# A hybrid decoder step on one core: packed low-rank products, one merged item per head pair, a centred output weight, and an order made anew

## The chip, the cores and the metric

The kernel runs on one core of one Trainium2 chip. The metric is the device time of one execution in microseconds (us). Five engines work side by side: TensorE (PE in the profile, its weight loads PEld), VectorE (DVE), ScalarE (ACT), GpSimd (POOL) and SyncE (SP, which issues nearly all DMA transfers). Each engine has its own list of instructions, in the order in which the program gives them, and instructions of different engines wait for each other by semaphores.

## The reference, cut to what matters

One layer of a decoder is applied to a prompt of 1024 tokens and to 8 single-token samples, all in float32. The projection, the two recurrent branches and the merge are:

```python
p = jnp.einsum('btd,dn->btn', x, w_in)                     # 1024 -> 3088 + 4224 + 2048 columns
q, k, v, g_a, a_lr = _split(p_gla, GLA_SPLITS)             # gated linear attention (GLA), 4 heads
o_gla, S_gla = _gla_chunked(...)                           # then RMS norm, times silu(g_a)
w = jnp.exp(-RWKV_DECAY_SCALE * jax.nn.sigmoid(rwkv_w0 + jnp.tanh(w_lr) @ rwkv_w2))
a = jax.nn.sigmoid(rwkv_a0 + aa_lr @ rwkv_a2)              # low-rank products, rank 64
y, S_rwkv = _rwkv7_scan(r, w, k, v, kk, a, S_rwkv0)        # 16 heads of 64, a recurrence over tokens
m = sigmoid(gate_a) * (o_gla @ w_up_gla) + sigmoid(gate_b) * (o_rwkv @ w_up_rwkv)
out = m @ w_out
y_out = _layernorm(DEEPNORM_ALPHA * x + out, ln_g, ln_b, LN_EPS)
```

The outputs are `y_out` for prompt and samples, and the new states of both branches.

## The kernel before, in words

**Arithmetic.** A product of the projection kind is made of three matmuls in the type `fp32r`: the activations and the weights are each split into a high part (a cast on ScalarE) and a low part (a subtraction, mostly on VectorE), and high*high, high*low and low*high are added up in one PSUM bank. The tiles are `xs` (activations) and `wpart` (weights). Smaller products are plain float32; the profile counts two records for one such matmul.

**Stages.** The prompt is cut into two passes: the first has 512 tokens and the 8 samples (token tiles of 256 and 264), the second 512 tokens. For each pass a list of "blocks" of 128 columns of `w_in` is projected; each block takes 24 matmuls for a token tile (8 slices of the contraction times 3). Between them stand the two branches: the RWKV branch works on pairs of heads (`pair`: `front`, `back`, `turn`, `chain`, `norm`), the GLA branch on heads (`gla_head`). Behind the projections come the up-projections with the gates (`up_row`), and last `out`: the product with `w_out` in tiles of 128 tokens by 512 columns (`out`), then the residual and the layer norm (`out_part`). The weights `w_out` are loaded and split ahead of that by `load_out`, from row 0 to row 1023 in eight slices.

**Places that the change touches.** `warm` issues two matmuls on a tile of zeros before the first load has landed. `run_all` holds the order of the first loads (`self.first`): `wa`, `x0`, `w0`, `x1` and so on, all on SyncE. `low_rank` makes the 16 columns of the GLA decay with `wa`, four slices of the contraction side by side in the array. `lora_sample` makes the samples' two low-rank products in two halves of 512 columns: four items, each one matmul with 64 rows and 8 columns, each with its own copy and store. In `back`, the inverse of a triangular block is merged in two products: `pA` (32 small matmuls) and `pZ` (4 matmuls, in the profile `big<-X,A`); `turn` then transposes the tiles b and k (16 transposes, `big<-cons,bk`) as an item of its own.

**Tiles of the array.** A matmul with few rows or columns uses only a part of the 128x128 array; the profile writes the part as rows*columns (128*32, 64*128).

**What sets the order.** A list scheduler in the kernel (`Order`) writes the instruction order of all engines when the program is built. Every piece of work is a generator ("stream") that offers one instruction, or one group of them (`together`), at a time; `price` gives each a duration, `HOP` the delay from one engine to another, `SWITCH` the price of another tiling of the array, and the stream whose next item can start first (less a priority) is written next. PSUM banks are taken from four classes: `proj` (2 banks), `big` (4), `pch` (1), `pY` (1). A new price moves instructions on all engines.

Of the kernel before, what the change touches and what calls it, by code (L numbers as in the profile page):

```python
# [20 lines left out]
P = 128  # L21
D = 1024
# [40 lines left out]
WARM = 2  # L63
# [3 lines left out]
HOP = {"P": 0.2, "D": 0.26, "G": 0.14, "V": 0.14, "A": 0.14}  # L67
# [78 lines left out]
def price(eng, name, out, args, ins):  # L146
# [3 lines left out]
    if eng == "P":  # L150
# [4 lines left out]
        if args[0].dtype == F32R:  # L155
            return max(m / 1200, n / 2165)
        if rows == cols == P:
            return 2 * max(m, n) / 1200 + 0.005
# [98 lines left out]
class Order:  # L257
# [4 lines left out]
    def __init__(self, nc):  # L262
        self.P, self.A, self.V, self.G, self.S, self.E, self.C = (Engine(**e) for e in (
            {"P": nc.tensor}, {"A": nc.scalar}, {"V": nc.vector}, {"G": nc.gpsimd}, {"S": nc.sync},
            {"V": nc.vector, "G": nc.gpsimd}, {"A": nc.scalar, "V": nc.vector}))
        self.tiles = (P, P)
# [157 lines left out]
class Kern(Order):  # L424
# [72 lines left out]
    def setup(self):  # L497
# [20 lines left out]
        nc.scalar.preload_act_table_set(EXP)  # L518
# [47 lines left out]
    def warm(self):  # L566

        z = self.kept["XT"][0]
        ps = yield from self.bank("big", [P, 512])
        for _ in range(WARM):  # L570
            yield self.P.matmul(ps, z[:, :P], z[:, :512], start=True, stop=True)
        self.free(ps)
# [41 lines left out]
    def load_x(self, src, i, wait=None, low_rank=False):  # L614
# [9 lines left out]
        def high():  # L624
            for k in range(NK):
                yield lambda: len(raws) > k
                h, lo = yield from self.get("xs", 2)
                yield self.A.copy(h[:, :n], raws[k])
# [3 lines left out]
        def low():  # L632
            for k in range(NK):
                yield lambda: len(his) > k
                yield self.E.tensor_sub(los[k], raws[k], his[k].bitcast(F32))
# [12 lines left out]

    def load_w(self):
# [5 lines left out]
        def high():  # L655
            n = 0
            while True:
                yield lambda: len(raws) > n
                w = yield from self.get("wpart")
                yield self.A.copy(w[:, 0], raws[n][0])  # L660
# [5 lines left out]
        def low():  # L666
            for n in range(count):
# [3 lines left out]
                yield self.E.tensor_sub(w[:, 1], raw, w[:, 0].bitcast(F32))  # L671
# [10 lines left out]
        for n, (src, c0, j, i) in enumerate(todo):  # L682
# [356 lines left out]
    def lora_sample(self, lw, l2s):  # L1039
        for hf, l2 in enumerate(l2s):  # L1040
            for q in range(2):
                rs = slice(64 * q, 64 * q + 64)
                pw = yield from self.bank("big", [NS, 512])
                yield self.P.matmul(pw, lw[rs, HT:], l2[rs], start=True, stop=True)
                wa = yield from self.row(512)
                yield self.A.copy(wa[:NS], pw)
                self.free(pw)
                yield self.S.dma_start(self.WA[q, :, 512 * hf:512 * hf + 512], wa[:NS])
                self.free(wa)
            self.free(l2)  # L1050
# [77 lines left out]
    def front(self, c, p, st, d):  # L1128
# [63 lines left out]
        for x in range(0, NCH, H):  # L1192
# [3 lines left out]
                            for n in range(H) for h, hs in enumerate(HS)])  # L1196
# [45 lines left out]
    def back(self, d):  # L1242
# [5 lines left out]
        for h in range(2):  # L1248
# [3 lines left out]
                                      start=True, stop=True) for n in range(2) for x in range(H) for h in range(2)], 2.0)  # L1252
# [4 lines left out]
        pZ = yield from self.bank("big", [P, H, 32])  # L1257
        yield together([self.P.matmul(pZ[q[g]], A_[:, q[g]], d.X2[:, g], start=True, stop=True) for g in range(4)])
# [6 lines left out]
        self.free(pZ, A_, d.X2)  # L1265

    def turn(self, d):

        bt = d.BK.rearrange("p c t -> p (c t)")[:, :2 * HT].rearrange("p (c h k) -> p c h k", c=NCH, h=2)
        pt = yield from self.get("big", 2)  # L1270
        yield together([self.tr(pt[h][:, x * C:x * C + C], d.BK[hs, x, h * C:h * C + P])
                        for x in range(NCH) for h, hs in enumerate(HS)])
# [14 lines left out]
    def chain(self, c, p, d):  # L1287
# [12 lines left out]
        for x in range(NCH):  # L1300
# [20 lines left out]
            for h, hs in enumerate(HS):  # L1321
# [3 lines left out]
                else:  # L1325
# [5 lines left out]
                        for x in range(first, NCH) for h, hs in enumerate(HS)], 0.5)  # L1331
        yield together([self.P.matmul(pY[h][HS[x % 2], x // 2], GG[:, x, 1, h], u_[:, x, h], start=False, stop=(x >= NCH - 2))
                        for h in range(2) for x in range(NCH)])
# [211 lines left out]
    def load_out(self):  # L1545
# [4 lines left out]
        for j in range(2):  # L1550
            for hf in range(2):
                yield self.S.dma_start(self.lnv[j][hf], self.a["ln"][j, 512 * hf:512 * hf + 512].partition_broadcast(P))
        for k in range(NK):
# [273 lines left out]
```

## Time and profile before

| | |
|---|---|
| time, median of 3 runs | 1467.58 us (1467.34 to 1470.01) |
| profiled execution | 1466.08 us |
| its span, first to last instruction | 1464.1 us |
| PE busy | 1443.8 us, 99% of the span |
| DVE, ACT, POOL busy | 1139.0, 888.7 and 77.7 us |
| DMA | 318.06 MB, mean 217 GB/s |

The profiled execution takes 2.0 us more than its span, which is what lies around the first and last instruction. In the profile's rows, `x8` counts instruction records, numbers behind a bar are busy time and the mean of one in ns, and `<-` in brackets names what ended the idle time before the row. In a timeline a row merges neighbouring instructions of one kind: its start, the time that it covers, and their count.

### The profile page before, as it was taken

What the parts mean: (1) busy time and instruction counts of PE and PEld (TensorE: products, weight loads), DVE (VectorE), ACT (ScalarE), POOL (GpSimd) and SP (SyncE); (2) the same over time, 40 slices, a digit from 0 to 9 for tenths busy, and PEclk for the clock granted to TensorE, in tenths of its full rate; (3) what the DMA queues carried; (4) which work ended last, traced back from release to release, by engine and by line L of the source; (5) the groups of instructions that cost most, each with busy time, mean ns of one, the idle gap of its engine ahead of it and who ended that gap; (6) DMA issues with size and microseconds to landing.
All of it is one profiled execution on the core that took longest, in us unless ns stands there. A gap on an engine that the chain in (4) does not pass through costs nothing. (4 is left out here: it accounts for less than half of the span.)

```text
span 1464.1 us, 32120 instructions
## 1 busy us (share of the span) xinstructions
PE 1443.8 (99%) x11670; PEld 1261.4 (86%) x11670; DVE 1139.0 (78%) x3022; ACT 888.7 (61%) x2356; POOL 77.7 (5%) x107
## 2 busy tenths in 40 slices
PE   9999999999999999999999999999999999999997
PEld 6999999999989998878888887878787899988786
DVE  6687879788988798877778898797876866755665
ACT  6666767777776776665855565566456746553210
POOL 0000000001100001000000010111000000000000
PEclk9999999999999999999999999999999999999999
DMA  9786887587767877667566556655564777896432
GB/s 314 275 276 212 265 285 233 198 282 267 230 226 233 281 237 240 209 193 224 151 188 209 156 187 205 201 140 187 181 180 138 251 221 244 294 319 230 131 113 82
DMA packets 201273, 318.06 MB, mean 217 GB/s; under 512 B 81827, under 2 KB 97068, under 8 KB 201116
## 3 DMA queue, kind: packets, MB, share of 16 engines
q1 hardware_dynamic: 201116, 316.01, 67.2%
q8 instruction: 93, 1.52, 0.4%
q14 instruction: 64, 0.52, 0.1%
HBM read 197.32 MB, written 118.61 MB: 216 GB/s over the span
## 5 line engine op out<-in xcount | busy, mean ns | idle before, releaser
L218 PE MATMUL proj<-xs,wpart 128*128 128x264 f32 (+2 forms) x5640 | 1018.3, 327 | 1.0 <-DVE row L218 0.8
L218 PEld LDWEIGHTS proj<-xs,wpart 128*128 128x128 f32 x5640 | 807.4, 189 | 78.6 <-issue 9.2
L218 ACT CAST wpart<-wraw 128x512 fp32r<-128x512 f32 x210 | 129.8, 623 | 85.1 <-PE big L218 37.2
L218 DVE TENSOR_TENSOR row<-row 128x512 f32<-128x512 f32 (+8 forms) x331 | 169.6, 521 | 8.3 <-ACT row L218 2.6
L218 DVE TENSOR_TENSOR wpart<-wraw,wpart 128x512 fp32r<-128x512 f32 x203 | 141.7, 700 | 34.5 <-ACT wpart L218 32.6
L218 ACT ACTIVATE row<-row 128x512 f32<-128x512 f32 (+5 forms) x197 | 119.0, 607 | 17.8 <-DVE row L218 8.2
L218 PE MATMUL big<-xs,wpart 128*128 128x512 f32 (+2 forms) x576 | 102.9, 332 | 0.3
L218 DVE TENSOR_TENSOR X<-X,Xt 128x60 f32<-128x60 f32 (+21 forms) x432 | 95.5, 221 | 9.2
L218 DVE TENSOR_TENSOR Xt<-X,wide 128x60 f32<-128x60 f32 (+21 forms) x432 | 91.5, 212 | 8.8
L218 PEld LDWEIGHTS big<-xs,wpart 128*128 128x128 f32 x576 | 87.0, 188 | 11.8 <-DVE xs L218 1.1
L218 ACT ACTIVATE row<-proj,omu 128x256 f32<-128x256 f32 (+1 forms) x99 | 54.1, 547 | 69.3 <-PE proj L218 68.7
L218 DVE SCALAR_TENSOR_TENSOR wide<-pch,pc,s0p 64x64 f32<-64x64 f32 x208 | 58.7, 282 | 45.5 <-PE pch L218 40.0
L218 POOL TENSOR_TENSOR row<-row 128x512 f32<-128x512 f32 (+6 forms) x46 | 49.9, 1090 | 631.2 <-DVE row L218 279.9
L218 ACT COPY rh<-pch 128x128 f32<-128x128 f32 x101 | 26.9, 266 | 79.6 <-PE pch L218 78.6
L218 DVE SCALAR_TENSOR_TENSOR row<-proj,pv,row 128x255 f32<-128x255 f32 (+1 forms) x99 | 56.4, 570 | 21.9 <-ACT tail L218 14.2
L402 ACT ACT_TABLE_LOAD x56 | 71.8, 1283 | 0.9
L218 ACT COPY row<-big 128x128 f32<-128x128 f32 (+7 forms) x141 | 40.9, 311 | 51.8 <-PE big L218 39.2
L218 PE MATMUL big<-row 128*32 128x32 f32 (+4 forms) x1068 | 67.9, 237 | 1.1 <-DVE row L218 0.5
L218 ACT COPY row<-wide 64x64 f32<-64x64 f32 x240 | 58.2, 242 | 3.1
L218 PEld LDWEIGHTS pch<-wide,gg 128*128 128x128 f32 x256 | 43.2, 188 | 12.1 <-PE proj L218 4.6
L218 PE MATMUL pch<-wide,gg 128*128 128x128 f32 x256 | 50.9, 280 | 2.0 <-DVE wide L218 1.3
L218 ACT ACTIVATE row<-proj 128x128 f32<-128x128 f32 (+4 forms) x136 | 37.1, 326 | 25.8 <-PE proj L218 24.9
(265 smaller groups left out, 1991.0 us busy)
## 6 DMA issues: line engine op xcount, KB each, us to landing
w<-wpart SPq DMA_DIRECT2D x146, 512.0 KB
wpart<-w SPq DMA_DIRECT2D x146, 512.0 KB
wraw<-w_in SPq DMA_DIRECT2D x146, 256.0 KB
wide<-LD SPq DMA_DIRECT2D x16, 512.0 KB
wraw<-w_up_gla SPq DMA_DIRECT2D x32, 256.0 KB
wraw<-w_up_rwkv SPq DMA_DIRECT2D x32, 256.0 KB
sg<-row SPq DMA_DIRECT2D x16, 260.0 KB
row<-sg SPq DMA_DIRECT2D x16, 260.0 KB
```

The costliest lines, as they stand in the source:

```text
L218: ways.append((eng, lambda call=call: call(out, *args, **kw), price(eng, name, out, args, ins)))
L402: self.nc.scalar.preload_act_table_set(self.table)
```

## The change

- **Low-rank products of the samples** (`lora_sample`): the four matmuls become one item of four matmuls that sit in different parts of the array (two halves of the rows, two groups of 32 columns). Each takes 32 columns instead of 8, of which the last 8 are used. There are two copies instead of four, and four stores as before.
- **Second merge product and transposes as one item** (`back`, `turn`): `pZ` and the 16 transposes are given to the scheduler as one group, which takes three banks of `big` at once. `turn` only copies the result.
- **Start**: the warm-up is one matmul of 512 and one of 256 columns instead of two of 512. The first weights (`w0`) are loaded by ScalarE's own queue, ahead of the activation table; `x0` is issued ahead of `wa` on SyncE. The first x tile and the first weight tile are split in two pieces each. The first two blocks may take PSUM banks of `pY` and `big` too.
- **End** (`load_out`, `out`, `residual`, `out_part`): each row of `w_out` has its mean subtracted when it is split, and the residual is scaled and its mean subtracted by a stream of its own as soon as x has landed, so the sum has mean zero without a subtraction of its own. The product with `ln_g` is made before the variance is known. In the last tile, ScalarE scales by the inverse deviation where GpSimd did, and GpSimd has one product and one sum left. `load_out` loads two slices of `w_out` ahead.
- **Prices of the scheduler**: `HOP` for VectorE 0.14 -> 0.21 and ScalarE 0.14 -> 0.22, ScalarE's fixed part 0.097 -> 0.04, small changes for PE, and factors on four groups (1.1, 2.7, 0.66, 1.17) and on the merged one (0.72).

```diff
-WARM = 2
+WARM = (512, 256)
-HOP = {"P": 0.2, "D": 0.26, "G": 0.14, "V": 0.14, "A": 0.14}
+HOP = {"P": 0.2, "D": 0.26, "G": 0.14, "V": 0.21, "A": 0.22}
...
-            return max(m / 1200, n / 2165)
+            return max(m / 1200, 0.005 + n / 2260)
...
-        return 0.097 + n / 1200 + (0.042 if len(src) == len(ins) else 0.0) + 0.094 * extra
+        return 0.04 + n / 1200 + (0.042 if len(src) == len(ins) else 0.0) + 0.094 * extra
...
-            yield from self.load(f"w{n}", self.S.dma_start(raw, src[c0 // P, j]))
+            yield from self.load(f"w{n}", (self.S if n else self.B).dma_start(raw, src[c0 // P, j]))
+            if not n:
+                self.nc.scalar.preload_act_table_set(EXP)
...
-                    banks.append((yield from (self.get("proj") if b.src is self.a["w_in"] else self.get_of("proj", "pY", "big"))))
+                    banks.append((yield from (self.get("proj") if b.src is self.a["w_in"] and at > 1 else self.get_of("proj", "pY", "big"))))
...
     def lora_sample(self, lw, l2s):
...
+        m = slice(HT + NS - 32, HT + NS)
+        pw = yield from self.get("big", 2)
+        yield together([self.P.matmul(pw[q][32 * hf:32 * hf + 32], lw[64 * q:64 * q + 64, m], l2s[hf][64 * q:64 * q + 64],
+                                      start=True, stop=True) for hf in range(2) for q in range(2)], 2.0)
...
-        pZ = yield from self.bank("big", [P, H, 32])
-        yield together([self.P.matmul(pZ[q[g]], A_[:, q[g]], d.X2[:, g], start=True, stop=True) for g in range(4)])
+        pZ_, *pt = yield from self.get("big", 3)
+        pZ = pZ_[:, :H * 32].rearrange("p (c t) -> p c t", t=32)
+        yield together([self.P.matmul(pZ[q[g]], A_[:, q[g]], d.X2[:, g], start=True, stop=True) for g in range(4)]
+                       + [self.tr(pt[h][:, x * C:x * C + C], d.BK[hs, x, h * C:h * C + P])
+                          for x in range(NCH) for h, hs in enumerate(HS)], 0.72)
...
+            for hf in range(2):
+                yield self.V.tensor_reduce(m[:, hf:hf + 1], raw[hf], mybir.AxisListType.X, ALU.add)
+            yield self.V.tensor_scalar(m[:, 2:3], m[:, 0:1], m[:, 1:2], -1.0 / D, ALU.add, ALU.mult)
...
-                yield self.A.copy(hi, raw)
-                yield self.E.tensor_sub(lo, raw, hi.bitcast(F32))
+                yield self.A.activation(hi, raw[hf], AF.Identity, bias=m[:, 2:3])
+                yield self.V.scalar_tensor_tensor(lo, raw[hf], m[:, 2:3], hi.bitcast(F32), ALU.add, ALU.subtract)
...
+    def residual(self, z, st, x0, w):
+        for j in range(2):
+            yield self.S.dma_start(z[j], self.a["x"][x0:x0 + w, 512 * j:512 * j + 512])
+        for j in range(2):
+            yield self.V.bn_stats(st[:, 6 * j:6 * j + 6], z[j])
+        yield self.V.bn_aggr(st[:, 24:26], st[:, :12])
+        yield self.V.tensor_scalar(st[:, 26:27], st[:, 24:25], -ALPHA, None, ALU.mult)
+        for j in range(2):
+            yield self.A.activation(z[j], z[j], AF.Identity, scale=ALPHA, bias=st[:, 26:27])
...
             if aside:
-                yield G.tensor_scalar(y, y, mv[:, 0:1], rs, ALU.subtract, ALU.mult)
-                yield G.tensor_mul(y, y, lw)
+                yield A.activation(y, y, AF.Copy, scale=rs)
                 yield G.tensor_add(y, y, lb)
             else:
-                yield V.scalar_tensor_tensor(y, y, mv[:, 0:1], lw, ALU.subtract, ALU.mult)
                 yield V.scalar_tensor_tensor(y, y, rs, lb, ALU.mult, ALU.add)
...
-        self.first = ["wa", "x0", "w0", "x1", "x2", "x3", "w1", "x4", "x5", "x6", "x7", "pv", "shift", "w2", "w3", "cst"]
+        self.first = ["x0", "w0", "wa", "x1", "x2", "x3", "w1", "x4", "x5", "x6", "x7", "pv", "shift", "w2", "w3", "cst"]
```

What this does to the order of the instructions is shown at three places.

TensorE, the samples' low-rank products (`big<-row 8x512`, each a quarter of them) in the first pass, before, among the projections (`proj`):

```order
L218 MATMUL proj<-xs,wpart 128x256
L218 MATMUL big<-row 8x512
L218 MATMUL proj<-xs,wpart 128x256 x9
L218 MATMUL big<-row 8x512
L218 MATMUL proj<-xs,wpart 128x256 x7
L218 MATMUL big<-row 8x512
```

The same place in the changed kernel:

```order
L218 MATMUL proj<-xs,wpart 128x264 x24
L218 MATMUL proj<-xs,wpart 128x256 x15
L218 MATMUL big<-row 32x512 x4
L218 MATMUL proj<-xs,wpart 128x256 x9
L218 MATMUL proj<-xs,wpart 128x264 x24
```

The four products stood apart, with 9, 7 and 17 projection matmuls between them; now they stand together, once.

TensorE, one head pair of the first pass, before: `X,gg` is the first merge product, `X,A` the second, `cons,bk` the transposes of b and k, `cons,row` those of v.

```order
L218 MATMUL proj<-xs,wpart 128x264 x9
L218 MATMUL big<-X_173,A 32x128 x4
L218 MATMUL proj<-xs,wpart 128x256 x11
L218 MATMUL big<-cons,bk 128x64 x16
L218 MATMUL proj<-xs,wpart 128x256 x3
L218 MATMUL big<-cons,row 128x128 x4
```

A head pair of the first pass in the changed kernel:

```order
L218 MATMUL big<-X_5208,gg 32x32 x16
L218 MATMUL proj<-xs,wpart 128x256 x11
L218 MATMUL big<-X_172,A 32x128 x4
L218 MATMUL big<-cons,bk 128x64 x16
L218 MATMUL proj<-xs,wpart 128x256
L218 MATMUL proj<-xs,wpart 128x264 x18
L218 MATMUL big<-cons,row 128x128 x4
```

The projections that stood between the second product and the transposes stand elsewhere; this holds for all 16 pairs.

VectorE, the last tile of the output (`XT` holds residual and sum, `az` the vectors of the layer norm, `st` the statistics), before:

```order
L218 SCALAR_TENSOR_TENSOR XT_169<-XT_169,proj 128x256
L218 BN_STATS st<-XT_169 128x6
L218 BN_AGGR st<-st 128x2
L218 SCALAR_TENSOR_TENSOR XT_169<-XT_169,st,az 128x512 x2
L218 SCALAR_TENSOR_TENSOR XT_169<-XT_169,st,az 128x256 x2
```

and in the changed kernel:

```order
L218 TENSOR_TENSOR XT_168<-XT_168,az 128x512
L218 BN_STATS st<-XT_168 128x6
L218 TENSOR_TENSOR XT_168<-XT_168,az 128x256
L218 BN_STATS st<-XT_168 128x6
L218 BN_AGGR st<-st 128x2
L218 SCALAR_TENSOR_TENSOR XT_168<-XT_168,st,az 128x512
L218 SCALAR_TENSOR_TENSOR XT_168<-XT_168,st,az 128x256
```

Behind the last statistics stood four instructions and stand two; the products with `az` (`ln_g`) have gone ahead of them.

More of the change, by code (lines that the diff above doesn't have):

```diff
@@ L569, in warm @@
         ps = yield from self.bank("big", [P, 512])
-        for _ in range(WARM):
-            yield self.P.matmul(ps, z[:, :P], z[:, :512], start=True, stop=True)
+        for n in WARM:
+            yield self.P.matmul(ps[:, :n], z[:, :P], z[:, :n], start=True, stop=True)
         self.free(ps)
@@ L627, in high @@
                 h, lo = yield from self.get("xs", 2)
-                yield self.A.copy(h[:, :n], raws[k])
+                for s in self.halves(k or i or not low_rank, HT // 2, n):
+                    yield self.A.copy(h[:, s], raws[k][:, s])
                 his.append(h[:, :n])
@@ L634, in low @@
                 yield lambda: len(his) > k
-                yield self.E.tensor_sub(los[k], raws[k], his[k].bitcast(F32))
+                for s in self.halves(k or i or not low_rank, HT // 2, n):
+                    yield self.E.tensor_sub(los[k][:, s], raws[k][:, s], his[k][:, s].bitcast(F32))
                 if not low_rank:
@@ L647, in load_x, with halves @@
             raws.append(raw)
+    def halves(self, later, at, n):
+        return [slice(0, n)] if later else [slice(0, at), slice(at, n)]
     def load_w(self):
@@ L659, in high @@
                 w = yield from self.get("wpart")
-                yield self.A.copy(w[:, 0], raws[n][0])
+                for s in self.halves(n, P, 4 * P):
+                    yield self.A.copy(w[:, 0, s], raws[n][0][:, s])
                 his.append(w)
@@ L1039, in lora_sample @@
     def lora_sample(self, lw, l2s):
[L1040 to L1050, printed above, removed]
+        m = slice(HT + NS - 32, HT + NS)
+        pw = yield from self.get("big", 2)
+        yield together([self.P.matmul(pw[q][32 * hf:32 * hf + 32], lw[64 * q:64 * q + 64, m], l2s[hf][64 * q:64 * q + 64],
+                                      start=True, stop=True) for hf in range(2) for q in range(2)], 2.0)
+        self.free(*l2s)
+        for q in range(2):
+            wa = yield from self.row(512)
+            yield self.A.copy(wa[:64], pw[q][:64])
+            self.free(pw[q])
+            for hf in range(2):
+                yield self.S.dma_start(self.WA[q, :, 512 * hf:512 * hf + 512], wa[32 * hf + 32 - NS:32 * hf + 32])
+            self.free(wa)
     def tails(self):
@@ L1264, in back @@
             yield self.C.copy(GG[hs, :, 0, h], d.AZ[hs, :, 0])
-        self.free(pZ, A_, d.X2)
+        self.free(pZ_, A_, d.X2)
+        d.pt = pt
     def turn(self, d):
         bt = d.BK.rearrange("p c t -> p (c t)")[:, :2 * HT].rearrange("p (c h k) -> p c h k", c=NCH, h=2)
-        pt = yield from self.get("big", 2)
-        yield together([self.tr(pt[h][:, x * C:x * C + C], d.BK[hs, x, h * C:h * C + P])
-                        for x in range(NCH) for h, hs in enumerate(HS)])
+        pt = d.pt
         for h in range(2):
@@ L1552, in load_out, with load @@
                 yield self.S.dma_start(self.lnv[j][hf], self.a["ln"][j, 512 * hf:512 * hf + 512].partition_broadcast(P))
+        raws = []
+        def load():
+            for k in range(NK):
+                yield lambda: k - len(self.wo) < 2
+                raw = yield from self.rows(2, 512)
+                for hf in range(2):
+                    yield self.S.dma_start(raw[hf], self.a["w_out"][k * P:(k + 1) * P, 512 * hf:512 * hf + 512])
+                raws.append(raw)
+        self.spawn(load(), "out")
         for k in range(NK):
@@ L1600, in out @@
             z = [z_[ro, :512], z_[ro, 512:]]
-            for j in range(2):
-                yield self.S.dma_start(z[j], self.a["x"][x0:x0 + w, 512 * j:512 * j + 512])
             st = yield from self.get("st")
+            self.spawn(self.residual(z, st[ro], x0, w), "evacuate")
             end = fin and c.i
@@ L1753, in run_all @@
         self.ups = 0
+        self.levelled = set()
         self.plan, self.xq, self.ws, self.wo, self.gts, self.l2s = [], [], [], [], [], []
```

40 lines of the change are left out of this document (26 added, 14 removed).

## The prediction

> **What bounds the kernel now.** I read the page's first part first:
>
> ```profile
> span 1464.1 us, 32120 instructions
> PE 1443.8 (99%) x11670; PEld 1261.4 (86%) x11670; DVE 1139.0 (78%) x3022; ACT 888.7 (61%) x2356; POOL 77.7 (5%) x107
> ```
>
> TensorE is busy 99% of the span; only 20.3 us are not covered by a matmul. So time can go in three ways only: fewer or cheaper matmuls, less waiting on TensorE, and less before its first and behind its last matmul. VectorE and ScalarE count where TensorE waits for them. What TensorE waited for stands in the view of waits (total us, times, longest); of its sixteen rows the ones that I use:
>
> ```profile
> PE big L218 <- POOL XT L563: 1.7, 1, 1.7
> PE pch L218 <- DVE wide L218: 1.6, 5, 0.4
> ...
> PE big L218 <- issue: 1.2, 1, 1.2
> ...
> PE proj L218 <- DVE row L218: 0.8, 1, 0.8
> ...
> PE big L218 <- DMA X<-XD: 0.5, 1, 0.5
> ...
> PE big L218 <- ACT bk L218: 0.2, 1, 0.2
> ```
>
> The sixteen add up to 11.4 us. The 1.7 and the 0.8 (of the block wait) belong to the start, so 8.9 us of waits are spread over the other 1440 us, none over 1.2. That is all that a better order can remove.
>
> **The change part by part.** *Samples' low-rank products.* The timeline of TensorE has one of the four items, and, much later, an item whose four matmuls of 512 columns already stand side by side (128*16, eight records):
>
> ```profile
> 27.36 1.02 PE L218 MATMUL big<-row 64*8 64x512 f32 x2
> 28.32 1.33 PE L218 MATMUL proj<-xs,wpart 128*128 128x256 f32 x9
> ...
> 590.35 1.05 PE L218 MATMUL big<-row,wa 128*16 128x512 f32 x8
> 591.33 0.39 PE L218 MATMUL proj<-xs,wpart 128*128 128x264 f32 x1
> ```
>
> One item keeps the projections off for 28.32 - 27.36 = 0.96 us; four of them take 3.84. Four matmuls packed by columns take 591.33 - 590.35 = 0.98, no more than one alone. The new item is packed by two column groups and two row halves. If both run side by side it costs 0.98 and saves 2.9 us; if the row halves take turns, 1.96, and it saves 1.9. I take 2.9: the transposes quoted next run in two row halves, and 16 of them fit into 0.65 us.
>
> *Second merge product and transposes as one item.* One pair, then a place where an item of the tiling 128*32 is already followed at once by the transposes, then dense matmuls of 256 columns:
>
> ```profile
> 254.90 0.42 PE L218 MATMUL big<-X,A 128*32 128x128 f32 x8
> 255.26 1.56 PE L218 MATMUL proj<-xs,wpart 128*128 128x256 f32 x11
> 256.74 0.71 PE L218 MATMUL big<-cons,bk 64*128 64x64 f32 x16
> 257.39 0.39 PE L218 MATMUL proj<-xs,wpart 128*128 128x256 f32 x1
> ...
> 192.96 0.64 PE L218 MATMUL big<-row 128*32 128x256 f32 x8
> 193.53 0.76 PE L218 MATMUL big<-cons,bk 64*128 64x64 f32 x16
> 194.22 0.44 PE L218 MATMUL big<-cons,S 128*128 128x128 f32 x2
> ...
> 1450.62 0.87 PE L218 MATMUL proj<-gg,xs 128*128 128x256 f32 x6
> 1451.34 0.52 PE L218 MATMUL proj<-wide,xs 128*128 128x256 f32 x3
> ```
>
> Dense matmuls of 256 columns follow each other after (1451.34 - 1450.62)/6 = 0.12 us. The eleven between the two items should take 1.32 and took 256.74 - 255.26 = 1.48: the return to the full array and the next departure cost 0.16 together. Merging removes one return and one departure per pair and puts one change of tiling between the two. The transposes take 257.39 - 256.74 = 0.65 behind projections and 194.22 - 193.53 = 0.69 behind another tiling, so that change is not free. I take 0.1 per pair, 1.6 us for 16; the ends are 0 (the inner change costs what both outer ones did) and 0.16, that is 2.6 us. Nothing is queued behind a new wait that was not there: the transposes need b and k, which are older than the product's operand. What is new is that three of the four `big` banks must be free at once; that is a rival below.
>
> *Start.* SyncE, ScalarE, VectorE and TensorE in the first 16 us:
>
> ```profile
> 0.74 0.38 SPq L218 DMA_DIRECT2D wa<-wa  x1
> 1.18 0.42 SPq L218 DMA_DIRECT2D row<-xT  x1
> 1.74 3.78 PE L218 MATMUL big<-XT 128*128 128x512 f32 x4 [1.74 <-POOL XT L563]
> 3.98 0.62 ACT L218 CAST xs<-row 128x520 fp32r<-128x520 f32 x1 [1.97 <-DMA row<-xT]
> 4.95 0.62 ACT L218 CAST wpart<-wraw 128x512 fp32r<-128x512 f32 x1 [0.34 <-DMA wraw<-w_in]
> 5.62 1.59 PE L218 MATMUL proj<-xs,wpart 128*128 128x256 f32 x7
> 7.14 1.37 PE L218 MATMUL big<-row,wa 128*16 128x256 f32 x16
> ...
> 12.86 1.31 DVE L218 TENSOR_TENSOR wpart<-wraw,wpart 128x512 fp32r<-128x512 f32 x2 [0.30 <-ACT wpart L218]
> 15.60 0.85 PE L218 MATMUL proj<-xs,wpart 128*128 128x256 f32 x5 [0.77 <-DVE row L218]
> ```
>
> The first projection at 5.62 waits for the cast of `w0` (4.95 + 0.62) and for the warm-up (1.74 + 3.78 = 5.52). With x0 one issue slot earlier (1.18 - 0.74 = 0.44), `w0` beside it from ScalarE's queue (issue and table load are over before the first cast at 3.98), and casts of a half and a quarter, it could start near 4.5. But the low-rank item at 7.14 waits for x1 to x3, which move by about one slot. I take 0.5 for this part; the ends are 0 and 1.1. The wait of 0.77 ahead of 15.60 is block 1 waiting for a `proj` bank; with banks of `pY` and `big` it goes, and what is late next is the split of `w2` and `w3`, done at 12.86 + 1.31 = 14.17, in time. I take 0.9 with the refill behind it, ends 0 and 0.9. Together 1.4 (0 to 2.0).
>
> *Weighing a rule.* The warm-up runs at half pace: its four records take 3.78/4 = 0.95 us each, where the two of the same width at 27.36 take 0.48, while the page's clock row shows nothing of it. The Trainium skill, "TensorE: Matmul & The Clock Gate", Part 1, says that the array's clock is halved until some 3.4 us of sustained work have passed, whatever the number of matmuls. The rows agree as far as they go: the old warm-up of 3.78 us is over that, and the projections behind it run at full pace. By that rule a warm-up of 512 and 256 columns, an estimated 2 x 0.95 + 2 x 0.48 = 2.9 us, leaves part of the first real work at half pace, and the sum would be up to 1.8 us smaller (the rival on the clock).
>
> *End.* Behind the last matmul, and the costs of single instructions there, with the nearest row for ScalarE's scaling of 256 columns:
>
> ```profile
> 1457.74 2.98 DVE L218 SCALAR_TENSOR_TENSOR XT<-XT,st,az 128x512 f32<-128x512 f32 x4
> 1458.07 0.20 ACT L218 ACTIVATE st<-st 128x1 f32<-128x1 f32 x1
> 1459.50 2.17 SPq L218 DMA_DIRECT2D y_p<-XT  x3
> 1459.70 1.61 POOL L218 TENSOR_TENSOR XT<-XT,az 128x256 f32<-128x256 f32 x2
> ...
> L218 DVE SCALAR_TENSOR_TENSOR XT<-XT,st,az 128x512 f32<-128x512 f32 x2 | 1.6, 806 | 0.1
> L218 DVE SCALAR_TENSOR_TENSOR XT<-XT,st,az 128x256 f32<-128x256 f32 x2 | 1.3, 650 | 0.0
> ...
> 14.50 0.47 ACT L218 ACTIVATE row<-proj,omu 128x256 f32<-128x256 f32 x1 [0.80 <-PE proj L218]
> ```
>
> GpSimd ends at 1459.70 + 1.61 = 1461.31 and the third store's issue at 1461.67; the span ends 2.4 us later. In the changed kernel the deviation is known at 1458.27; VectorE's two instructions end at 1459.1 and 1459.75; ScalarE (0.47) and one GpSimd sum (1.61/2 = 0.8) end at 1459.55. Three issues of 0.43 each from 1459.1 end at 1460.4: 1.3 us saved (0.8 if GpSimd and VectorE hinder each other more, 1.8 if the issues overlap).
>
> *The rest costs nothing on TensorE's path.* The mean of `w_out` adds 16 reductions and 8 small instructions on VectorE, the residual stream one statistic per half tile; a pass over 512 columns takes 0.69, and the table loads grow by 8 of 1.28:
>
> ```profile
> 1434.82 0.69 DVE L218 BATCH_NORM_STATS2 st<-XT 128x6 f32<-128x512 f32 x1
> L402 ACT ACT_TABLE_LOAD x56 | 71.8, 1283 | 0.9
> ```
>
> VectorE gains about 16 x 0.69 = 11 us of work in the last 200 us and ScalarE 10 us overall; their idle shares (22% and 39%) cover it. Without cover it would delay the first output tile by one slice of `w_out`, 2 us.
>
> *The new order.* A new set of prices moves waits about. VectorE's later hand-over (0.07) speaks against the five `pch` waits; a place behind a swap of activations where two chain matmuls now stand with nothing between them speaks for one new wait of about 1 us. I take 1 us saved of the 8.9, with ends of 8.9 saved and 6 lost.
>
> Sum: 2.9 + 1.6 + 1.4 + 1.3 + 1.0 = 8.2 us. Against the profiled execution (1464.1 of span and 2.0 around it, 1466.1) that gives 1457.9. The median of the runs shown lies 1.5 us above that execution, so I forecast 1459 for the median.
>
> **The rivals.**
> - *The new order is worth far more than 1 us.* For it: the waits are many, small and of one kind. Against it: 8.9 us is the ceiling. With 6 of 8.9 saved and the merge at 2.6, the sum is 14.2: 1453.
> - *The new order gives back what the parts save.* TensorE's list is full and every place has moved; the waits would have to grow from 8.9 to about 15. For it: the new wait named above. Against it: the longest now is 1.2, and projections stand around nearly every item. With 6 lost instead of 1 saved the sum is 1.2: 1466, no change that can be told.
> - *Slower: the merged item stands in TensorE's list without its banks or its operand.* Three of four `big` banks at once must be emptied by ScalarE and VectorE, and the projections behind wait with it, 16 times. Without its own 1.6 the rest saves 6.6, so it breaks even at 0.41 us per pair and is slower by 0.2% (2.9 us) from 0.6. For it: the product already waits for its operand once (0.5, `X<-XD`). Against it: once in 16, and no wait on a copy of these banks exceeds 0.2 (the last row of the waits). At 0.75 per pair 12 us are lost against 6.6: 1473.
> - *The clock.* First real work at half pace: 7 projections of 0.12 and a low-rank item of about 1 us double, 1.8 us at most: 1461.
>
> **How the numbers follow.** Forecast 0.54, larger gain 0.20, clock 0.08, given back 0.12, slower 0.06. The likeliest gives 1459; its own range is 1456 to 1462. For 8 in 10 the range reaches to 1452 below (most of the larger gain) and 1465 above (part of "given back"). About 0.2%, 2.9 us, is what a measurement of this kernel tells from no change: faster means below 1464.7, which holds for the first three cases and a third of the fourth: 0.86; within 0.09; slower 0.05.
>
> **What would show it.** Right: TensorE's waits at or below 9 us behind the first 20 us; one `big<-row` item of 64*32 of about 1 us in place of four; `X,A` and `cons,bk` together within 1.1 us, 16 times; dense projections from about 14 us on; 6 us instead of 7.6 from the last matmul to the end. Wrong: more idle time on TensorE with `big` banks or `X,A` named, first projections 0.24 apart, or an unchanged end.

## The result, and the profile after

The changed kernel takes 1458.46 us (median of six executions, 1457.09 to 1461.04), the kernel before beside it 1467.46 (six, 1466.38 to 1470.18): a ratio of 0.9942 with a 95% interval of 0.9932 to 0.9951. That is 8.5 us faster by the ratio, and 9.0 between the two medians. The forecast was 1459, from 1452 to 1465. The profiled execution took 1461.04, the longest of the six.

The page of the changed kernel, span and first part:

```profile
span 1458.9 us, 32139 instructions
PE 1437.7 (99%) x11670; PEld 1261.6 (86%) x11670; DVE 1136.0 (78%) x3005; ACT 926.4 (64%) x2468; POOL 68.8 (5%) x100
```

TensorE is still the bound: 1437.7 us busy instead of 1443.8, with 21.2 us not covered instead of 20.3. Its view of waits (total us, times, longest) has twelve rows, of which these:

```profile
PE big L218 <- DVE xs L218: 2.0, 4, 0.8
PE pch L218 <- DVE wide L218: 1.8, 3, 0.8
PE big L218 <- POOL XT L563: 1.7, 1, 1.7
...
PE proj L218 <- ACT wpart L218: 0.7, 1, 0.7
PE big L218 <- ACT bk L218: 0.6, 1, 0.6
```

The twelve add up to 11.3 us; without the 1.7 and the 0.7 of the start 8.9 are left, as much as before. The last row is a bank of a merged item: once, behind the first head pair, TensorE waits 0.6 us until ScalarE has copied the transposes out of it (`bk<-big`). That row was 0.2 before. The samples' low-rank item and one merged item in TensorE's timeline:

```profile
29.32 1.06 PE L218 MATMUL big<-row 64*32 64x512 f32 x8
30.31 3.88 PE L218 MATMUL proj<-xs,wpart 128*128 128x256 f32 x30
...
246.72 0.43 PE L218 MATMUL big<-X,A 128*32 128x128 f32 x8
247.08 0.71 PE L218 MATMUL big<-cons,bk 64*128 64x64 f32 x16
247.72 1.34 PE L218 MATMUL proj<-xs,wpart 128*128 128x264 f32 x9
```

All four low-rank products keep the projections off for 30.31 - 29.32 = 0.99 us, as long as one of them did before. A merged item takes 247.72 - 246.72 = 1.00. The start, on TensorE and ScalarE:

```profile
1.74 2.93 PE L218 MATMUL big<-XT 128*128 128x512 f32 x4 [1.74 <-POOL XT L563]
5.37 1.74 PE L218 MATMUL proj<-xs,wpart 128*128 128x256 f32 x6 [0.70 <-ACT wpart L218]
7.03 2.40 PE L218 MATMUL big<-row,wa 128*16 128x256 f32 x16
9.36 3.56 PE L218 MATMUL proj<-xs,wpart 128*128 128x256 f32 x25
...
16.01 1.23 PE L218 MATMUL pY<-xs,wpart 128*128 128x256 f32 x9
...
4.40 0.72 ACT L218 CAST xs<-row 128x256 fp32r<-128x256 f32 x2 [1.95 <-DMA row<-xT]
5.02 0.71 ACT L218 CAST wpart<-wraw 128x128 fp32r<-128x128 f32 x2
```

The first cast begins at 4.40, later than before (3.98), though x0 was issued 0.45 earlier. Block 1 (now in `pY`, without a wait) begins at 16.01, later than before (15.60): its bank wait is gone, and something else has eaten more than that. The end, first the last matmul and VectorE's instructions behind it in the kernel before, then all of it in the changed kernel:

```profile
1455.97 0.52 PE L218 MATMUL proj<-wpart,xs 128*128 128x256 f32 x3
1456.53 0.42 DVE L218 SCALAR_TENSOR_TENSOR XT<-XT,proj 128x256 f32<-128x256 f32 x1 [1.97 <-PE proj L218]
...
1457.45 0.26 DVE L218 BATCH_NORM_AGGREGATE st<-st 128x2 f32<-128x24 f32 x1
```

```profile
1449.52 0.52 PE L218 MATMUL proj<-wpart,xs 128*128 128x256 f32 x3
1450.08 0.42 DVE L218 TENSOR_TENSOR XT<-XT,proj 128x256 f32<-128x256 f32 x1 [2.34 <-PE proj L218]
1450.42 0.75 DVE L218 BATCH_NORM_STATS2 st<-XT 128x6 f32<-128x256 f32 x2
1451.20 0.69 DVE L218 TENSOR_TENSOR XT<-XT,az 128x512 f32<-128x512 f32 x1
1451.81 0.42 DVE L218 BATCH_NORM_STATS2 st<-XT 128x6 f32<-128x256 f32 x1
1452.26 0.42 DVE L218 TENSOR_TENSOR XT<-XT,az 128x256 f32<-128x256 f32 x1
1452.60 0.42 DVE L218 BATCH_NORM_STATS2 st<-XT 128x6 f32<-128x256 f32 x1
1453.06 0.26 DVE L218 BATCH_NORM_AGGREGATE st<-st 128x2 f32<-128x24 f32 x1
...
1453.97 1.65 DVE L218 SCALAR_TENSOR_TENSOR XT<-XT,st,az 128x512 f32<-128x512 f32 x2 [0.66 <-ACT st L218]
...
1454.75 1.74 SPq L218 DMA_DIRECT2D y_p<-XT  x3
```

From the last matmul's end (1449.52 + 0.52 = 1450.04) to the end of the span 8.9 us pass; before it was 7.6 (from 1455.97 + 0.52 = 1456.49). VectorE idled for 2.34 us ahead of the last part's sum, and only behind it come four statistics and two products; all of these but one statistic belong to parts that were summed before.

So the gain lies in the middle. From block 1's first matmul to the last matmul's end the kernel before takes 1456.49 - 15.60 = 1440.9 us and this one 1434.0: 6.9 less. The start gives back 0.4 of that and the end 1.3.

### The profile page after: what moved, and what is told of

Its sections match the earlier page's. It is cut to its first block, busy times and chain, and to the rows that moved or that the text cites. A ratio compares the mean times of both kernels' runs of the same rounds, so it can differ in the third digit from the quotient of the medians.

```text
span 1458.9 us, 32139 instructions
## 1 busy us (share of the span) xinstructions
PE 1437.7 (99%) x11670; PEld 1261.6 (86%) x11670; DVE 1136.0 (78%) x3005; ACT 926.4 (64%) x2468; POOL 68.8 (5%) x100
## 3 DMA queue, kind: packets, MB, share of 16 engines
q8 instruction: 93, 1.52, 0.4%
## 4 chain that ended last, share of the span: by engine, by line
PE 82%; DVE 7%; ACT 6%; DMA 2%; issue 2%; SPq 0%; DVEq 0%; ACTq 0%
PE proj L218 51%; PE big L218 21%; PE pch L218 6%; PE pY L218 4%; DVE row L218 3%; ACT row L218 3%; DVE X L218 1%; ACT L403 1%; DVE Xt L218 1%; ACT wpart L218 1%; DMA row<-vd 1%; DVE wide L218 0%; SPq L218 0%; DMA wraw<-w_in 0%; DMA row<-o_rwkv 0%
## 5 line engine op out<-in xcount | busy, mean ns | idle before, releaser
L218 PE MATMUL proj<-xs,wpart 128*128 128x264 f32 (+2 forms) x5592 | 1008.0, 327 | 0.7 <-ACT wpart L218 0.7
L218 DVE TENSOR_TENSOR row<-row 128x512 f32<-128x512 f32 (+5 forms) x330 | 169.6, 520 | 7.9 <-ACT row L218 2.3
L218 ACT CAST wpart<-wraw 128x512 fp32r<-128x512 f32 (+1 forms) x211 | 130.1, 620 | 71.3 <-PE proj L218 31.3
L218 DVE TENSOR_TENSOR wpart<-wraw,wpart 128x512 fp32r<-128x512 f32 (+1 forms) x205 | 141.4, 691 | 34.0 <-ACT wpart L218 29.4
L218 ACT ACTIVATE row<-row 128x512 f32<-128x512 f32 (+4 forms) x197 | 118.8, 609 | 24.9 <-DVE row L218 13.7
L218 PE MATMUL big<-xs,wpart 128*128 128x512 f32 (+2 forms) x624 | 109.1, 329 | 2.5 <-DVE xs L218 2.0
L218 PEld LDWEIGHTS big<-xs,wpart 128*128 128x128 f32 x624 | 92.7, 188 | 15.3 <-DVE xs L218 3.6
L218 POOL TENSOR_TENSOR row<-row 128x512 f32<-128x512 f32 (+7 forms) x43 | 44.2, 1031 | 663.1 <-ACT row L218 208.3
L218 ACT COPY wide<-pch 64x64 f32<-64x64 f32 x206 | 42.3, 205 | 16.1 <-PE pch L218 12.2
L218 PEld LDWEIGHTS pch<-wide,gg 128*128 128x128 f32 x256 | 42.6, 188 | 11.3 <-PE proj L218 2.7
```

What stands on the lines that cost most here:

```text
L218: ways.append((eng, lambda call=call: call(out, *args, **kw), price(eng, name, out, args, ins)))
```

## The experiments

All were timed in five rounds beside the kernel before (medians 1466.08, 1465.91 and 1466.41 us in three jobs). The table has for each the median (executions), and from its profiled execution the three pieces: block 1's first matmul, the middle as above, and the end behind the last matmul, in us. Where one edit was to be tested alone, the order of all other instructions was kept as in the changed kernel. The four kernels of the last rows ran in another job than the changed kernel (1465.91 for the kernel before there; 1467.46 and 1466.08 in the changed kernel's two), so their distance from it is given both by the medians and by the ratios to the kernel before.

| kernel | median | block 1 at | middle | end |
|---|---|---|---|---|
| before | 1467.46 (6) | 15.60 | 1440.9 | 7.6 |
| changed | 1458.46 (6) | 16.01 | 1434.0 | 8.9 |
| changed, run again | 1458.95 (5) | 14.84 | 1431.6 | 8.9 |
| long warm-up | 1458.34 (5) | 15.07 | 1432.6 | 8.9 |
| end's list turned | 1457.48 (5) | 16.24 | 1432.1 | 6.9 |
| both | 1455.68 (5) | 14.24 | 1433.3 | 6.9 |
| both, again | 1456.82 (5) | 14.56 | 1432.9 | 6.8 |
| both, first weights from SyncE | 1456.55 (5) | 15.73 | 1431.3 | 6.8 |
| both, warm-up earlier and longer | 1456.31 (5) | 14.36 | 1432.6 | 6.8 |
| merged item apart | 1460.41 (5) | 16.41 | 1433.0 | 8.9 |
| low-rank matmuls apart | 1462.84 (11) | 14.48 | 1437.8 | 8.9 |
| old prices | 1460.46 (5) | 14.55 | 1437.3 | 7.0 |
| prices alone, on the kernel before | 1469.13 (9) | 16.52 | 1443.8 | 7.6 |

The eight rows from "changed" down to "warm-up earlier and longer" have the same instructions in the middle, but their single executions read 1431.3 to 1434.0 (mean 1432.6): a difference of a microsecond there is nothing. Against that mean the change is worth 8.3 us in the middle; the 1440.9 of the kernel before is a single execution too.

**Run again.** No edit.

> The changed kernel once more, as the standard for the next three. Median 1458.5 within 1.5 us, ratio to before 0.994. Its first profiled execution (1461.0 us) was the slowest of six, 2.6 us over their median. If the 8.2 us of the prediction are real, the second profile shows a sum near it; if only the 5.2 us between the two spans are real, this one also lies near 1461.

1458.95 us, ratio 0.9950 (0.9936 to 0.9963). The span of the profiled execution is 1455.4 us, 8.7 below that of the kernel before. The end is 8.9 again, so it belongs to the program. The start differs by 1.2 us with the same instructions.

**Long warm-up** (as many columns as before):

```diff
-            yield self.P.matmul(ps[:, :n], z[:, :P], z[:, :n], start=True, stop=True)
+            op = self.P.matmul(ps[:, :n], z[:, :P], z[:, :n], start=True, stop=True)
+            if n < 512:
+                more, fn = self.P.matmul(ps[:, n:2 * n], z[:, :P], z[:, n:2 * n], start=True, stop=True), op.fn
+                op.ways = [(op.eng, lambda: [fn(), more.fn()], op.cost)]
+            yield op
```

> The changed kernel with one warm-up matmul of 256 columns more, so that the warm-up is as long as before; the scheduler is not told of it, so every engine's order is otherwise that of the changed kernel. Theory of the clock (first real work at half pace because the warm-up was cut): the first projections stand 0.12 apart instead of 0.22, the first low-rank item takes 1.3 us instead of 2.3, dense projections begin at about 8.3 us instead of 9.36, and the whole is 1.0 to 1.5 us faster than the changed kernel. Theory of the loads (the landing of x1 to x3 sets the start, as the prediction had it): the first projections are quicker but dense work begins at 9 us or later, less than 0.4 us gained.

1458.34 us, ratio 0.9947 (0.9934 to 0.9959): not to be told from the changed kernel by itself, where 1.0 to 1.5 us were expected. Nor did the expected rows come: the first six projections still took 7.03 - 5.37 = 1.66 us, the low-rank item 8.74 - 7.03 = 1.71, and block 1 began at 15.07. What the warm-up does shows only over many executions, below.

**The end's list turned.** The last part's sum is given to VectorE only once the three other parts have their sums, statistics and products:

```diff
+        if parts == 3:
+            yield lambda: self.parted == n
...
+            self.parted += parts == 3
```

> The changed kernel, but in the last output tile VectorE adds a part only when the statistics and the product of the part before it are written; all else as in the changed kernel. Theory of the list (the last sum, which waits for the last matmul, stands ahead of older work in VectorE's list): the aggregate follows the start of the last matmul group after 1.5 us as before the change, instead of 3.5, and the end comes 2.0 us earlier, about 6 us behind the last matmul instead of 8.9. Rival (the stores, or GpSimd's two products, set the end): VectorE is done earlier but the span shrinks by less than 0.7 us.

1457.48 us, ratio 0.9941 (0.9929 to 0.9954). Its timeline:

```profile
1447.83 0.52 PE L218 MATMUL proj<-wpart,xs 128*128 128x256 f32 x3
1448.38 0.42 DVE L218 TENSOR_TENSOR XT<-XT,proj 128x256 f32<-128x256 f32 x1 [1.42 <-PE proj L218]
1448.84 0.43 DVE L218 BATCH_NORM_STATS2 st<-XT 128x6 f32<-128x256 f32 x1
1449.30 0.26 DVE L218 BATCH_NORM_AGGREGATE st<-st 128x2 f32<-128x24 f32 x1
...
1450.22 1.65 DVE L218 SCALAR_TENSOR_TENSOR XT<-XT,st,az 128x512 f32<-128x512 f32 x2 [0.66 <-ACT st L218]
...
1451.00 1.74 SPq L218 DMA_DIRECT2D y_p<-XT  x3
```

The aggregate begins 0.95 us behind the last matmul's end (1448.35) instead of 3.02; in the kernel before it was 0.96. The end shrinks from 8.9 to 6.9. That the list was the cause of the long end is shown. The median moves by less, 1.0 to 1.5 where 2.0 were expected. The profiled execution had a late start (16.24), but no row tells how the four others began, so why the median moves by less stays open.

**Both edits,** the longer warm-up and the turned list.

> Both edits in one kernel. If start and end are independent, as a kernel bound by one engine's list would have it, the gains add up: 3.0 to 3.5 us faster than the changed kernel, about 1455. If the time won at the start is given back by waits for weights in the next blocks, only the end's 2.0 us remain.

1455.68 us, ratio 0.9930 (0.9917 to 0.9942); run again in the last job 1456.82, ratio 0.9943:

> The kernel with the longer warm-up and the end's list put in the other order, run once more as the standard of this job. If its gain is real, its median is 1455.7 us give or take 1 and its ratio to the kernel before 0.993. If that median was a lucky draw, it comes back between the two single edits, 1457.5 to 1458.3.

The second run missed the expected median by 0.1, and its ratio is that of the end's edit alone (0.9941), so it settles neither expectation. The ten executions together have a median of 1456.3 us, the eleven of the changed kernel 1458.5, and eight of the ten lie below the fastest of the eleven: about 2.2 us better than the change, and faster than both kernels.

**First weights from SyncE,** behind x0 instead of beside it (which puts `wa` third):

```diff
-            yield from self.load(f"w{n}", (self.S if n else self.B).dma_start(raw, src[c0 // P, j]))
+            yield from self.load(f"w{n}", self.S.dma_start(raw, src[c0 // P, j]))
```

> As the standard of this job, with the first weights issued by SyncE behind x0 instead of by ScalarE's queue beside it; the order is otherwise unchanged. Theory (transfers side by side slow each other): x0's first cast starts near 3.6 to 4.0 us instead of 4.40, the cast of the first weights does not start before 5.0, so the first projection moves by less than 0.4 us and the time by less than 0.5. Rival (x0's landing has nothing to do with what runs beside it): the cast of x0 stays at 4.3 to 4.5, the first weights land about 0.45 us later, and so do the first projection and the end.

ScalarE's timeline here:

```profile
3.49 0.72 ACT L218 CAST xs<-row 128x256 fp32r<-128x256 f32 x2 [1.47 <-DMA row<-xT]
4.13 0.71 ACT L218 CAST wpart<-wraw 128x128 fp32r<-128x128 f32 x2
6.28 0.62 ACT L218 CAST xs<-row 128x520 fp32r<-128x520 f32 x1 [1.45 <-DMA row<-xT]
```

and in the kernel with both edits, run again beside it, where the two loads start together:

```profile
4.43 0.72 ACT L218 CAST xs<-row 128x256 fp32r<-128x256 f32 x2 [1.99 <-DMA row<-xT]
5.05 0.71 ACT L218 CAST wpart<-wraw 128x128 fp32r<-128x128 f32 x2
```

With the loads one behind the other x0's first cast begins 0.9 us earlier, and that of the weights right behind it at 4.13, not after 5.0 as was expected, though they were issued 0.46 later (1.19 instead of 0.73). When they land beside x0 no row shows, only that they are there by 5.05. What x0 loses, 0.9 us, it loses to what runs beside it. The Trainium skill, "DMA: Bandwidth & Descriptors", section "Issuing engines are not separate DMA queues", says that transfers of all issuing engines run on the same 16 DMA engines and interleave; these rows agree. Nothing came of it in the time (1456.55 against 1456.82): x1 is now the late one, its cast begins at 6.28 instead of 5.67, and block 1 at 15.73 instead of 14.56. Part of that is TensorE's clock, granted in full from 6.8 us here and from 5.4 there (more on it below).

**Warm-up earlier and longer** (the zeroing of the tile that it reads is cut in two, and it has 256 more columns):

```diff
-                nc.gpsimd.memset(t, 0.0)
+                for s in ([slice(0, 512), slice(512, 1024)] if tag == "XT" and not n else [slice(None)]):
+                    nc.gpsimd.memset(t[:, s], 0.0)
```

> As the standard of this job, with the zeroing of the tile that the warm-up reads cut in two, so that the warm-up starts near 1.3 instead of 1.74 us, and with 256 more columns of warm-up. Theory (the array's pace turns full some time after work begins, and the moment differs between executions): the first low-rank item takes 1.3 us as at full pace and block 1 begins near 14.2; the median is the same as the standard's or up to 0.5 us lower, with a smaller spread. Rival (more warm-up columns only push the first projection back): the first projection starts at 5.6 or later and the median is up to 0.5 us higher.

1456.31 us (1455.65 to 1456.53), ratio 0.9936 (0.9923 to 0.9949), the smallest spread of the three kernels timed together. The low-rank item took 1.00 us, block 1 began at 14.36. The first projections were still slow (5.34 to 7.03 for six).

**Merged item apart.** The transposes are written behind the next four projections (`op` of the merged item issues its first four matmuls, the rest follows later):

```diff
+            self.late.append([5, lambda: [f() for f in parts[1]], {x.tensor.name for x in pt}])
+        op.ways = [(op.eng, fn, op.cost)]
```

> The changed kernel, but the 16 transposes of each pair are written four TensorE items (mostly projection matmuls) behind the second merge product instead of at once behind it; the scheduler is not told, so all other instructions keep their order. The prediction's size of the merge (0.1 us per pair): 1.6 us slower than the changed kernel. The size read from the trace after (a merged item costs about 1.19 us with its returns, the two apart 0.56 + 0.84 = 1.40): 3.2 us slower. If the merge saves nothing in itself: same time.

1460.41 us, ratio 0.9962 (0.9949 to 0.9976). The same pair as above:

```profile
246.90 0.42 PE L218 MATMUL big<-X,A 128*32 128x128 f32 x8
247.26 0.76 PE L218 MATMUL proj<-xs,wpart 128*128 128x264 f32 x4
247.94 0.71 PE L218 MATMUL big<-cons,bk 64*128 64x64 f32 x16
248.58 0.86 PE L218 MATMUL proj<-xs,wpart 128*128 128x264 f32 x5
```

The two items alone take 0.36 + 0.64 = 1.00 us, just what the merged one takes: the inner change of tiling costs no more than one from projections. The gain is in what lies around them: the four projections between take 0.68 where dense ones of 0.12 take 0.48. That is 0.20 per pair, 3.2 for 16. By the medians the edit costs 1.5 to 1.9 us, by the ratios 1.8 to 2.9, and the middle of its one profiled execution is only 0.4 above the mean. What merging is worth stays open between 1.5 and 3.2.

**Low-rank matmuls apart,** the same four with two projections between each:

```diff
+            fns[0]()
+            for n, f in enumerate(fns[1:]):
+                self.late.append([2 + (n == 0), f, {x.tensor.name for x in (*pw, *l2s, lw)}])
```

> The changed kernel, but the four packed low-rank matmuls of the samples have two projection matmuls between each two of them; all else in the same order. The prediction (packing saves 2.9 us because four run side by side in the time of one): about 2.9 us slower, 0.96 us for each of the four in TensorE's timeline. Rival (most of the saving came from fewer copies and waits): less than 1 us slower.

1462.84 us, ratio 0.9978 (0.9970 to 0.9987).

```profile
27.80 1.04 PE L218 MATMUL big<-row 64*32 64x512 f32 x2
28.77 0.51 PE L218 MATMUL proj<-xs,wpart 128*128 128x256 f32 x2
29.20 1.04 PE L218 MATMUL big<-row 64*32 64x512 f32 x2
...
32.99 5.55 PE L218 MATMUL proj<-xs,wpart 128*128 128x256 f32 x44
```

Each alone takes 28.77 - 27.80 = 0.97 us, and the two projections behind it 0.43 instead of 0.24. From 27.80 to 32.99 are 5.19 us; less six projections of 0.12, 4.47, against 0.99 for the packed item: packing is worth 3.5 us. The medians say 3.9 to 4.4 and the ratios 4.1 to 5.3. The middle of this execution is 5.2 above the mean, but 1.7 of that is no price of the edit: behind two waits of 0.83 and 0.71 us the trace grants TensorE 0.50 of its clock from 1202.75 to 1206.16, and what takes 3.41 us at half pace takes 1.7 less at full. The 3.5 that are left agree with the item.

**Old prices** (all of the change but the scheduler's prices and factors):

```diff
-HOP = {"P": 0.2, "D": 0.26, "G": 0.14, "V": 0.21, "A": 0.22}
+HOP = {"P": 0.2, "D": 0.26, "G": 0.14, "V": 0.14, "A": 0.14}
...
-        return 0.04 + n / 1200 + (0.042 if len(src) == len(ins) else 0.0) + 0.094 * extra
+        return 0.097 + n / 1200 + (0.042 if len(src) == len(ins) else 0.0) + 0.094 * extra
```

> The changed kernel with the scheduler's old prices: hand-overs, ScalarE's fixed part, PE's prices and the factors of the groups (the merged one 1 instead of 0.72). The prediction (the new prices are worth 1.0 us): 1459.5, that is 1 us slower than the changed kernel. Rival (the order is most of what lies beyond the parts): 3 us or more slower, with TensorE's waits well above 9 us.

1460.46 us, ratio 0.9963 (0.9950 to 0.9975). TensorE's waits add up to 15.6 us, and the first of them is

```profile
PE pch L218 <- DVE wide L218: 4.3, 6, 1.1
```

The changed kernel's add up to 11.3, and to 9.9 in its second run, so the new prices take 4 to 6 us off the waits (the middle says 1437.3 - 1432.6 = 4.7). They lose 2 at the end, where the old ones wrote VectorE's list in the better order (7.0). Net 1.5 to 2.0 by the medians, 1.9 to 3.1 by the ratios.

**Prices alone,** on the kernel before, without the merged item's factor:

> The kernel before with the new prices only (all but the factor of the merged item, which it does not have). The prediction: 1.0 us faster than before. Rival (the order is most of what lies beyond the parts): 3 us or more faster. If a new set of prices is one draw among many: anything from 4 us faster to 4 us slower, with the difference in TensorE's waits.

1469.13 us, ratio 1.0023 (1.0013 to 1.0033): slower by 3.2. The waits there add up to 14.6, with another row on top:

```profile
PE big L218 <- DVE S L218: 3.1, 5, 0.8
```

The same prices that save waits in one program add them in another. What they bring belongs to the order that came out, not to the prices.

**The pace at the start, over all profiles.** The timelines show for each execution from when TensorE keeps its full pace (projections 0.12 us apart instead of 0.22, or the matmuls of the low-rank item as close as in its later copies), in us:

```
warm-up of 768 columns:   6.0  6.1  6.1  |  10.0  10.7  11.3
warm-up of 1024 or more:  6.1  6.2  6.6  6.6  7.0  7.9
```

(The run with the first weights from SyncE is left out: at the moment in question it waited for x1.) With the short warm-up three of six executions stay at half pace 4 to 5 us longer. In these block 1 begins at 16.0 to 16.4, in the other three at 14.5 to 14.8: 1.6 us between their means. None of the six with a longer warm-up did that.

The traces also hold the moment from which the full clock was granted, which the views average away: 4.7, 5.2 and 5.3 us, and 10.0, 10.6 and 11.2, with the short warm-up; 5.4 to 7.9 with a longer one. (The first projections are 0.22 apart for some other reason too: in the execution with the full clock from 4.7 they are so until 6.1.) In all thirteen profiled executions the stretch at full clock that begins there lasts a whole number of times 3.413 us, 423 times in the changed kernel. So the clock is set once in 3.413 us here, at a phase of its own. Counted back in such windows, TensorE was busy for at least 80.7% of the last window before the full clock, and for at most 79.5% of the one before that (time ahead of the program counted as idle). In the three late executions this refused window holds the pause of 0.7 to 0.9 us between the short warm-up and the first projection (79.5, 74.6 and 79.5% busy); the longer warm-up leaves next to no pause. The Trainium skill, "TensorE: Matmul & The Clock Gate", Part 1, says that the clock follows the activity in a window of about 3.4 us that runs on its own, so that the moment of full pace varies from run to run; these traces agree, with 3.413 us.

How often the start is late is a count over six executions with the short warm-up and six with a longer one, not an interval. In the times, the longer warm-up is worth 0.6 us without the end's edit (1458.95 to 1458.34) and 1.2 with it (1457.48 to 1456.3), each within the uncertainty.

## Why the prediction was right, and where it was not

The sum (8.2) and the forecast (1459) hold: 1458.46. It held partly by luck, because errors cancel: the middle saved more than was forecast, start and end together saved nothing.

- **Samples' low-rank products, 2.9:** right mechanism, the size too small. The item is 0.99 us as forecast, the row halves do run side by side. What it saves is 3.5, because the sum counted 0.96 per item by the first projection's start and left out the return to the full array (0.43 - 0.24 = 0.19 behind each), which the second part of the same prediction did count.
- **Merged item, 1.6:** right in kind and within what can be measured (1.5 to 3.2). I put an inner change of tiling at a third of the saving; the rows show none. The slower rival (the item waits for three banks) did not come: by the groups of the changed kernel, the idle time ahead of these items is 0.1 us in all, where it was 1.7. Its banks hold up another item once, for the 0.6 us of the row `bk`.

```profile
L218 PE MATMUL big<-cons,bk 64*128 64x64 f32 x256 | 11.4, 228 | 0.0
L218 PE MATMUL big<-X,A 128*32 128x128 f32 x128 | 7.1, 285 | 0.1
```

- **Start, 1.4 saved:** failed as a step; the changed kernel lost 0.4 in its first profiled execution and gained 0.8 in the second. The bank wait went, as said. "The first projection near 4.5" was wrong: x0 lands 0.9 us later beside `w0`, so the first cast starts at 4.4 and the first projection at 5.37. And the rival on the clock came true in half of the profiled executions with the short warm-up; it was priced at up to 1.8 and costs 1.6. It had a chance of 0.08; by these runs it was nearer a half. I also gave a wrong reason: "the projections behind it run at full pace" does not follow from seven projections in 7.14 - 5.62 = 1.52 us, which is 0.22 each. The clock record of that trace has full clock from 5.81, so it was true of the clock, but these rows did not show it. With the long warm-up block 1 begins 0.5 to 1.4 us earlier than in the kernel before, so the term's size was to be had.
- **End, 1.3 saved:** wrong sign, 1.3 lost. The step assumed that the deviation is known as soon behind the last matmul as before and looked only at the instructions behind the aggregate. The rows ahead of it in VectorE's list, which the order of the changed kernel had on show, put the last sum in front of the other parts' statistics and products. With the list turned the end saves 7.6 - 6.9 = 0.7, about the lower bound given: VectorE's pair takes 1.65 us beside GpSimd, where I had 0.81 and 0.65, and the three store issues 1.74 instead of 1.3.
- **New order, 1.0:** right in sign, too small: 1.5 to 3.1 in exchange for the old prices. The reason given, fewer waits of `pch`, holds against the old prices (4.3 us there, 1.8 here) and not against the kernel before (1.6). As the same prices cost the kernel before 3.2 us, the sign was partly luck. The profile's sum of waits alone would have hidden it, 8.9 before and after; with the old prices the new program waits for 13.2 (15.6 with the start).
- **"The rest costs nothing on TensorE's path":** true, but the loads were wrong. VectorE fell from 1139.0 to 1136.0 us instead of gaining 11, and ScalarE gained 38 instead of 10: with its fixed part priced lower the scheduler gave it copies that VectorE had (`wide<-pch` went from 176 to 206, `rh<-pch` from 101 to 116). The prices account for about half: with the old ones ScalarE is busy for 906.2 us, between 888.7 before and 926.4. The eight table loads are there (64 instead of 56).

By terms, for the middle: 3.5 for the low-rank products, 1.5 to 3.2 for the merge, and the 1.6 to 3.3 that are left of 8.3 for the order and what was not measured. The middle with the old prices puts the order at 4.7, more than is left. So either the merge is at its lower end (its own middle said 0.4), or the terms do not simply add. Of the signs listed, the waits, the one low-rank item and the merged item came as said; the end did not, and first projections 0.22 apart, a sign of being wrong, came too. The sum of 5.5 that I had for the middle was 2.8 short; start and end, which were to save 2.7, lost 1.7 in the profiled execution and 0.5 in the one run again.

## What to carry to other kernels

Where an engine writes its list in order, read the whole list from the last operand's arrival backwards: a wait placed ahead of work that is ready costs that work's whole length at the end (2.0 us here). Count a partial-array item by the time until the projections are back at their pace, not by its own length; 0.2 us a visit lay in the return. And a first load that starts together with another one can land later (0.9 us here): put the one that is wanted first alone in front, and ask what then becomes the late one. A warm-up has to last until the first real work is ready: a pause of 0.7 to 0.9 us cost 1.6 us whenever it fell into the window in which the clock was decided.

## What the runs showed that I had not expected

- The start of the same program has two outcomes: with a warm-up of 768 columns TensorE is at full pace from about 6 us or from 10 to 11, which moves block 1 by 1.6 us; with 1024 or more it always came by 7.9.
- A load of 260 KB that was issued together with another (256 KB, from another engine) let its first cast begin at 4.4 us; ahead of it, alone, at 3.5.
- The middle of the same program, some 1432 us of TensorE's list, read 1431.3 to 1434.0 from one execution to the next. Between the two executions of the changed kernel (1434.0 and 1431.6) three waits make up most of the difference. At 839.8 us it is 0.9: at 837.2 GpSimd began an instruction (1.30 us) just ahead of one of VectorE's (`az<-row,nkk`), which then took 1.79 us; in the other execution VectorE began first and took 0.75, and GpSimd's took 1.84. At 1209 and 1217 it is 0.5 each, behind loads (`o_rwkv`, `w_up_rwkv`) for which ScalarE waited 0.97 and 2.02 us instead of 0.44 and 0.93.
- The clock can fall in the middle of a program: in one of thirteen profiled executions (low-rank matmuls apart), behind a window in which TensorE was busy for 55%, the granted clock was 0.50 for 3.41 us.
